# Norm factors inside the matmul operands, 512-column gate and up products and token-major z and down in the second block of a two-block transformer

## Chip, cores and metric

The kernel runs on one NeuronCore of one Trainium2 chip. The time is device microseconds of one execution. The engines are TensorE (PE, its weight loads shown apart as PEld), VectorE (DVE), ScalarE (ACT), GpSimd (POOL) and SyncE (SP), which only issues transfers here.

## The reference, cut to what matters

x has 256 tokens of 1024 channels. A first block (convolution, sparse attention, pooling, a mixture of 32 experts) makes the x that enters the second block. The change touches the second block alone:

```python
def second_block(x, c, ...):
    mod = (silu(c) @ w_ada + b_ada)
    shift1, scale1, gate1, shift2, scale2, gate2 = split(mod, 6)
    h = rms_norm(x, norm1_w) * (1.0 + scale1) + shift1
    x = x + gate1 * hybrid_mixer(h, ...)
    h = rms_norm(x, norm2_w) * (1.0 + scale2) + shift2
    x = x + gate2 * ((silu(h @ w_gate) * (h @ w_up)) @ w_down)     # D_FF = 2816
    return rms_norm(x, norm_f_w)

def hybrid_mixer(h, w_in, ...):
    p = h @ w_in
    q, k, v = split(silu(causal_depthwise_conv(p[qkv], conv_qkv_w)))  # 4 taps, 3 x 512 channels
    o = gated_delta_rule_chunked(l2_normalize(q), l2_normalize(k), v, g, beta)  # 4 heads of 128
    y_gdn = rms_norm(o, gdn_norm_w) * silu(z)                         # 512 channels
    y_sc = sc_b * causal_depthwise_conv(sc_c * sc_h, conv_short_w)    # 3 taps, 512 channels
    return concatenate([y_gdn, y_sc]) @ w_out
```

## The kernel before, in words

The whole program is one straight list of instructions. It is written in program order with tiles from pools; a scheduler orders each engine's instructions at build time by their place in the program and by its own estimate of when operands and buffers are ready, and sets all semaphores. So an engine may work on a later part of the program (a z product) while an earlier part (the delta rule) waits, but on the chip each engine keeps the order that was fixed.

Weights come through a ring of SBUF tiles of 2 MB, four of them in the second block, issued in a fixed list by SP (`pump`, L144). Six tables of modulation weights of the second block come apart from this: `ada_cols` (L1474) loads eight pieces of 512 KB into two buffers and multiplies each with the condition vector in 8 small matmuls (L1481).

Activations lie with channels on the partitions and the 256 tokens along the free dimension. Products are made in a split precision: a weight w is written as wH + wL, an activation h as hH + hL, each rounded to the fp32r type that TensorE passes once, and a product is wH hH + wL hH + wH hL. `split` (L325) makes wH by a ScalarE copy (L331) and wL by a VectorE subtraction (L332) for 128 x 512 weights at a time, with three buffers each. `prodT` (L335) makes 128 output channels for 256 tokens out of 8 slices of 128 input channels: 24 matmuls (L342, L343, L345).

The norm is a factor per token and is kept out of the operand. `scaled` (L1235) writes hH and hL of x times the channel's gain G alone; two more columns (256 and 257) hold the shift, so one product gives both the unscaled result and the shift's contribution as a column of its own. The rows of the norm factor (`rrow`, `r4row`) are multiplied onto the results on VectorE, and the shift's column is added as a bias. This is why the matmuls have 258 columns.

The mixer: `conv_silu` (L1319) makes a chunk of 128 channels of q, k or v, twelve in all. Its product lies in one of three PSUM banks `zb`; VectorE multiplies it with `rrow` into the SBUF tile `pad` (L1327), which frees the bank, and the four taps work on `pad` (L1329 ScalarE, L1331 three times VectorE); L1333 is the SiLU. The second half of each chunk's wL goes to GpSimd (`low`, L1317), as do the squares of q and k (L1355), the masked copies of the triangular inverse (L1421), one tap of the short convolution (L1598) and the low halves of the mixed operand (L1552). `rowed` (L1336) does the same for z, c, h and b, four chunks each; z is transposed to tokens afterwards (L1540). The output projection runs in two halves (`fours`, L1607) with `down` (L347), 8 blocks of 24 matmuls of 256 columns, whose moving operand is the activation.

The feed-forward part: 22 blocks of 128 hidden channels. Each makes gate and up by `prodT` (L1644, L1645) into a PSUM bank `gb` each (four of them), the hidden tile by L1658 to L1663, its split by L1666 (ScalarE) and L1667 (GpSimd), and the `down` of the block before (L1670) into four PSUM banks that hold the output with channels on the partitions. The norm factor of the second norm is worked out beside the first gate and up products (L1646 to L1655). The table for gate2 is loaded and multiplied when f is 1024 (L1640). At the end the output is added to the residual, squared, transposed back to tokens (L1689), scaled by the last norm factor (L1710, L1712) and sent out (L1713). `rsqrt` (L254) is a VectorE operation and a power on GpSimd (L257).

## Time and profile before

| what | value |
|---|---|
| median of 3 runs | 1054.34 us (1054.06 to 1055.30) |
| the profiled execution, own time | 1055.91 us |
| its span in the profile | 1053.5 us |
| TensorE busy | 871.7 us, 83% of the span |
| VectorE, ScalarE, GpSimd busy | 435.0, 328.7, 84.5 us |
| mean granted TensorE clock | 0.904 of 2.4 GHz |

The span is the time from the first to the last instruction in the profile. Busy time is the time in which an engine has at least one instruction under way. Matmuls are pipelined: a matmul of 281 ns can start 118 ns after the one before it, so the distance of starts, not the duration, tells what a matmul costs in a row of them. Columns called "idle before" name what ended the idle time.

### The profile page before, as it was taken

What the parts mean: (1) busy time and instruction counts of PE and PEld (TensorE: products, weight loads), DVE (VectorE), ACT (ScalarE), POOL (GpSimd) and SP (SyncE); (2) the same over time, 40 slices, a digit from 0 to 9 for tenths busy, and PEclk for the clock granted to TensorE, in tenths of its full rate; (3) what the DMA queues carried; (4) which work ended last, traced back from release to release, by engine and by line L of the source; (5) the groups of instructions that cost most, each with busy time, mean ns of one, the idle gap of its engine ahead of it and who ended that gap; (6) DMA issues with size and microseconds to landing.
All of it is one profiled execution on the core that took longest, in us unless ns stands there. A gap on an engine that the chain in (4) does not pass through costs nothing. (4 is left out here: it accounts for less than half of the span.)

```text
span 1053.5 us, 20710 instructions
## 1 busy us (share of the span) xinstructions
PE 871.7 (83%) x8762; PEld 635.0 (60%) x8763; DVE 435.0 (41%) x1068; ACT 328.7 (31%) x722; POOL 84.5 (8%) x109
## 2 busy tenths in 40 slices
PE   4999986986677676666665768979999999999998
PEld 3776675653333342333332326768868989989997
DVE  2599846210110010000000106585557666656665
ACT  4442744210100010000000004643425555445554
POOL 0000002000000000000000002351013010000001
PEclk9899998998888787787786888989999999999998
DMA  9999935799999999999999999422535716545521
GB/s 352 427 426 418 413 135 240 304 421 423 419 421 423 424 419 421 423 422 423 420 422 422 418 421 406 157 95 96 194 128 219 299 44 240 208 175 218 200 81 40
DMA packets 38145, 322.82 MB, mean 306 GB/s; under 512 B 4256, under 2 KB 4640, under 8 KB 9760
## 3 DMA queue, kind: packets, MB, share of 16 engines
q1 hardware_dynamic: 37584, 320.64, 74.9%
q8 instruction: 70, 1.15, 0.4%
q0 software_dynamic: 176, 0.53, 0.1%
q10 hardware_dynamic: 288, 0.29, 0.1%
q14 instruction: 27, 0.22, 0.1%
HBM read 320.38 MB, written 1.05 MB: 305 GB/s over the span
## 5 line engine op out<-in xcount | busy, mean ns | idle before, releaser
L332 DVE TENSOR_TENSOR wL<-ring,wH 128x512 fp32r<-128x512 f32 (+1 forms) x212 | 146.7, 695 | 98.6 <-ACT wH L331 98.3
L331 ACT ACTIVATE wH<-ring 128x512 fp32r<-128x512 f32 (+1 forms) x224 | 137.1, 615 | 156.4 <-PE gb L345 67.1
L1066 PE MATMUL yy<-ring,aT 128*32 128x256 f32 x992 | 95.2, 544 | 38.5 <-DMA ring<-w 38.5
L1054 DVE TENSOR_TENSOR at<-sl,hh 128x128 f32<-128x128 f32 x32 | 9.1, 285 | 243.7 <-ACT sl L1052 243.7
L1035 PE MATMUL hh<-ring,px 128*32 128x256 f32 x1024 | 75.8, 423 | 31.2 <-DMA ring<-w 30.6
L1035 PE MATMUL hh<-ring,XT 128*32 128x256 f32 x1024 | 73.6, 411 | 26.1 <-DMA ring<-w 26.0
L1066 PEld LDWEIGHTS yy<-ring,aT 128*32 128x32 f32 x992 | 43.1, 149 | 77.6 <-issue 66.0
L343 PE MATMUL gb<-mixH,wL 128*128 128x258 f32 x352 | 89.4, 285 | 0.0
L342 PE MATMUL gb<-mixH,wH 128*128 128x258 f32 x352 | 89.3, 285 | 0.0
L1035 PEld LDWEIGHTS hh<-ring,px 128*32 128x32 f32 x1024 | 31.4, 119 | 67.9 <-DMA ring<-w 43.4
L1052 ACT ACTIVATE sl<-hh 128x128 f32<-128x128 f32 x32 | 8.9, 278 | 196.7 <-PE hh L1035 196.7
L1035 PEld LDWEIGHTS hh<-ring,XT 128*32 128x32 f32 x1024 | 32.6, 116 | 59.0 <-DMA ring<-w 33.0
L343 PEld LDWEIGHTS gb<-mixH,wL 128*128 128x128 f32 x352 | 66.6, 189 | 2.5 <-issue 2.1
L342 PEld LDWEIGHTS gb<-mixH,wH 128*128 128x128 f32 x352 | 66.8, 190 | 0.8 <-ACT mixH L1236 0.8
L1072 ACT ACTIVATE px<-yy 128x256 f32<-128x256 f32 x32 | 12.3, 385 | 162.3 <-PE yy L1066 162.3
L342 PE MATMUL zb<-mixH,wH 128*128 128x258 f32 x224 | 61.1, 301 | 1.2 <-DVE pad L1327 0.6
L343 PE MATMUL zb<-mixH,wL 128*128 128x258 f32 x224 | 59.6, 293 | 0.0
L345 PE MATMUL gb<-mixL,wH 128*128 128x258 f32 x352 | 56.7, 283 | 0.0
L1048 DVE COPY MT<-tm 128x256 f32<-128x256 f32 x32 | 13.6, 424 | 98.7 <-PE tm L1046 98.7
L345 PEld LDWEIGHTS gb<-mixL,wH 128*128 128x128 f32 x352 | 48.3, 189 | 0.0
L354 PE MATMUL zb<-dd,wH 128*128 128x256 f32 x264 | 47.8, 281 | 0.0
L342 PEld LDWEIGHTS zb<-mixH,wH 128*128 128x128 f32 x224 | 44.2, 198 | 5.6 <-issue 2.1
(532 smaller groups left out, 1623.6 us busy)
## 6 DMA issues: line engine op xcount, KB each, us to landing
ring<-w SPq DMA_DIRECT2D x132, 1024.0 KB, 22.4
ring<-wall SPq DMA_DIRECT2D x35, 2048.0 KB, 10.1
ring<-w SPq DMA_DIRECT2D x29, 2048.0 KB, 24.7
ring<-wall SPq DMA_DIRECT2D x21, 1024.0 KB, 15.4
aw<-w_ada SPq DMA_DIRECT2D x32, 512.0 KB, 4.2
px<-w SPq DMA_DIRECT2D x1, 2048.0 KB, 8.2
ring<-wall SPq DMA_DIRECT2D x1, 1600.0 KB, 25.7
ring<-wall SPq DMA_DIRECT2D x1, 1536.0 KB, 25.2
```

Of the source, the lines that this page charges most:

```text
L331: nc.scalar.activation(d[0], src, AF.Copy)
L332: eng.tensor_sub(d[1], src, d[0])
L342: nc.tensor.matmul(ps, wH[:, k], h[0][:, q + k], start=(q + k == 0), stop=False)
L343: nc.tensor.matmul(ps, wL[:, k], h[0][:, q + k], start=False, stop=False)
L345: nc.tensor.matmul(ps, wH[:, k], h[1][:, q + k], start=False, stop=(q + k == 7))
L354: nc.tensor.matmul(pss[k // 2][:, 256 * (k % 2):256 * (k % 2) + 256], lw[:, c], rh, start=first and i == 0 and k % 2 == 0, stop=last and i ...
L1035: nc.tensor.matmul(ps[32 * j:32 * j + 32], XT[e // 8][:, k, e % 8, :], w[:, k % 4, :, 128 * j:128 * j + 128], start=(k == 0), stop=(k == 7))
L1048: nc.vector.tensor_copy(MT[e], ps)
L1052: nc.scalar.activation(sl, ps[:, 0], AF.Silu)
L1054: nc.vector.tensor_mul(at, sl, ps[:, 1])
L1066: nc.tensor.matmul(ps[32 * j:32 * j + 32], aT[:, 32 * c:32 * c + 32], w[:, c, 256 * j:256 * j + 256], start=(c == 0), stop=(c == 3))
L1072: nc.scalar.activation(YS[e], ps, AF.Copy)
```

## The change

- The norm factor goes into the operands: `normed` forms t = x G r (r a row per token out of PSUM) on VectorE, hH = t + S on ScalarE and hL on VectorE. Operands have 256 columns, hH and hL lie side by side, and `rrow`, `r4row`, the shift's column and all that repaired the results are gone. The two norm factors must be known before the first product of q, k and v, and of gate and up.
- `prod` (mixer) keeps 24 matmuls of 256 columns; for the first two chunks of k both products run side by side. `prod_wide` (gate and up) multiplies wH with hH and hL in one matmul of 512 columns (8), and wL with hH in one of 256 (8); the two halves of the bank are added afterwards (a ScalarE copy, a VectorE sum).
- z and the feed-forward output are made with tokens on the partitions: the activation is the weight side and 512 channels of wH or wL move. The residual is transposed to tokens inside the loop (f = 512), the gate2 row and the final norm's row are spread over the partitions ahead of the loop, and the table for gate2 is multiplied there too.
- The taps of q, k and v read the product's PSUM bank directly. The work of GpSimd named above goes to VectorE or ScalarE. `split` has six buffers in the second block instead of three, the hidden tile three instead of two. The memory of the operand tiles is freed with the first block.

```diff
-    split, prodT, down = tools(t2)
+    split, down = tools(t2, 6)
...
+    def prod_wide(pss, ws, y):
+        for q in range(2):
+            v = [split(w[:, 4 * q:4 * q + 4], 4, 128) for w in ws]
+            for k in range(4):
+                for ps, (wH, wL) in zip(pss, v):
+                    nc.tensor.matmul(ps.rearrange("p (x t) -> p x t", x=2), wH[:, k], y[q][:, :, k],
+                                     start=(q + k == 0), stop=(4 * q + k == 7), skip_group_check=True)
+            for k in range(4):
+                for ps, (wH, wL) in zip(pss, v):
+                    nc.tensor.matmul(ps[:, 0:256], wL[:, k], y[q][:, 0, k], start=False, stop=(4 * q + k == 7),
+                                     skip_group_check=True)
+
+    def normed(y, xT, G, S, rows):
+        for k in range(8):
+            t = q1("nt")
+            nc.vector.scalar_tensor_tensor(t, xT[:, k], G[:, k:k + 1], rows, op0=OP.mult, op1=OP.mult)
+            h, l = (y[k // 4][:, n, k % 4] for n in range(2))
+            nc.scalar.activation(h, t, AF.Identity, bias=S[:, k:k + 1])
+            nc.vector.scalar_tensor_tensor(l, t, S[:, k:k + 1], h, op0=OP.add, op1=OP.subtract)
...
+    def conv_silu(dst, ps, chunk):
         cv = q1("cv")
-        nc.scalar.activation(cv, pad[:, 3:], AF.Copy, scale=P("cqkv", 4 * chunk + 3))
-        for t in range(3):
-            nc.vector.scalar_tensor_tensor(cv, pad[:, t:t + 256], P("cqkv", 4 * chunk + t), cv,
+        nc.scalar.activation(cv, ps, AF.Copy, scale=P("cqkv", 4 * chunk + 3))
+        for t in (2, 1, 0):
+            nc.vector.scalar_tensor_tensor(cv[:, 3 - t:], ps[:, 0:253 + t], P("cqkv", 4 * chunk + t), cv[:, 3 - t:],
...
-            nc.gpsimd.tensor_mul(sqh.rearrange("p (a t) -> p a t", a=2), raw[n][:, :, h], raw[n][:, :, h])
+            nc.scalar.activation(sqh.rearrange("p (a t) -> p a t", a=2), raw[n][:, :, h], AF.Square)
...
-        nc.gpsimd.tensor_mul(Ls, LT, GK("mT")[:, None, 64 * lev:64 * lev + 64].to_broadcast([128, 8, 64]))
+        nc.vector.tensor_mul(Ls, LT, GK("mT")[:, None, 64 * lev:64 * lev + 64].to_broadcast([128, 8, 64]))
...
+    pss = [zb(), zb()]
+    for k in range(8):
+        wH, wL = split(wz[:, k], 1, 512)
+        for a in range(2):
+                r = slice(128 * a, 128 * a + 128)
+                h, l = (y3[k // 4][:, n, k % 4, r] for n in range(2))
+                nc.tensor.matmul(pss[a], h, wH, start=(k == 0), stop=False)
+                nc.tensor.matmul(pss[a], l, wH, start=False, stop=False)
+                nc.tensor.matmul(pss[a], h, wL, start=False, stop=(k == 7))
...
-        nc.gpsimd.tensor_sub(mview(mL, k), src, mview(mH, k))
+        nc.vector.tensor_sub(mview(mL, k), src, mview(mH, k))
...
+    r4 = t2.tile([128, 2], F32, name="r4")
+    rsqrt(r4, pst[:, 0:2], 1.0 / D)
+    tok_row(pst[:, 256:512], r4)
+    y4 = ytiles()
+    normed(y4, x3T, G4, S4, pst[:, 256:512])
...
+    R = ada_sums(5120, ps)
...
     for f in range(0, 2816, 512):
-        if f == 1024:
-            ada_cols(5120, gt2, P("ab2", 8, 8), gb)
...
-            prodT(pg[:, 0:258], wg, 128 * j, y4)
-            prodT(pu[:, 0:258], wu, 128 * j, y4)
...
+                prod_wide([pg], [wg[:, :, c]], y4)
+                prod_wide([pu], [wu[:, :, c]], y4)
...
+            nc.scalar.activation(low[:, 0:256], pg[:, 256:512], AF.Copy)
+            nc.vector.tensor_add(tg, pg[:, 0:256], low[:, 0:256])
+            nc.scalar.activation(tg, tg, AF.Silu)
+            nc.scalar.activation(low[:, 256:512], pu[:, 256:512], AF.Copy)
+            nc.vector.tensor_add(tu, pu[:, 0:256], low[:, 256:512])
+            nc.vector.tensor_mul(hd, tu, tg)
...
-            nc.gpsimd.tensor_sub(dL, hd, dH)
...
+            nc.vector.tensor_sub(dd[:, 256:512], hd, dd[:, 0:256])
...
+    for a in range(2):
+        for c in range(2):
+            for n, (_, d) in enumerate(pend):
+                down2(halves_[n], d, a, c, False, n == 1)
+            r = slice(512 * c, 512 * c + 512)
...
+            nc.vector.tensor_mul(t, acc[a][c], gtr[:, r])
+            nc.vector.tensor_add(x4[a][:, r], x4[a][:, r], t)
...
+            nc.scalar.activation(t, x4[a][:, r], AF.Square, accum_out=ss5[:, a, c:c + 1])
+        nc.vector.tensor_add(r5[:, a:a + 1], ss5[:, a, 0:1], ss5[:, a, 1:2])
+        rsqrt(r5[:, a:a + 1], r5[:, a:a + 1], 1.0 / D)
...
+            nc.vector.scalar_tensor_tensor(x4[a][:, r], x4[a][:, r], r5[:, a:a + 1], nfr[:, r],
+                                           op0=OP.mult, op1=OP.mult)
+            nc.sync.dma_start(outv[:, a, r], x4[a][:, r])
```

## Rows read from the trace of the kernel before

**Rows 1.** The page, busy time of an engine (share of the span) and instructions.
```profile
PE 871.7 (83%) x8762; PEld 635.0 (60%) x8763; DVE 435.0 (41%) x1068; ACT 328.7 (31%) x722; POOL 84.5 (8%) x109
```
**Rows 2.** Busy time of each engine in stretches of the second block.
```profile
core 0: us, PE busy (x) PEld busy (x) DVE busy (x) ACT busy (x) POOL busy (x), PEclk, DMA share, GB/s
640.00:658.00 18.00, 16.10 (x128) 13.24 (x121) 13.86 (x49) 9.58 (x23) 6.32 (x5) 0.81 0.95 398
658.00:724.00 66.00, 56.07 (x676) 47.88 (x678) 45.45 (x96) 36.31 (x85) 28.08 (x24) 0.95 0.29 108
724.00:840.50 116.50, 116.50 (x1090) 96.77 (x1080) 69.58 (x160) 49.33 (x105) 13.96 (x18) 1.00 0.56 202
840.50:854.50 14.00, 12.31 (x97) 10.24 (x96) 9.39 (x24) 7.60 (x17) 1.54 (x2) 1.00 0.34 130
906.00:945.00 39.00, 39.00 (x333) 33.90 (x332) 21.54 (x44) 17.38 (x31) 2.94 (x4) 1.00 0.60 234
945.00:1039.50 94.50, 94.50 (x789) 94.50 (x789) 62.02 (x121) 50.25 (x88) 7.76 (x11) 1.00 0.39 145
```
**Rows 3.** TensorE: timeline, one line's matmuls, and the chain (start us, us, what).
```profile
110.62 1.03 PE L690 MATMUL bank<-kvT,qaT 128*128 128x256 f32 x4
...
L1149 PE MATMUL pb<-par,S x16: 256/256/276, 644.5 to 646.2; 128*128 128x8 f32 x16
...
644.50 1.95 PE L1149 MATMUL pb<-par,S 128*128 128x8 f32 x16
...
L633 PE MATMUL bank<-cqT,ring x16: 379/379/483, 102.3 to 106.4; 128*128 128x256 f32 x16
...
L354 PE MATMUL zb<-dd,wH 128*128 128x256 f32 x264 | 47.8, 281 | 0.0
...
857.33 1.66 PE zb L354 x14
```
**Rows 4.** Groups of VectorE and ScalarE in 945 to 1039.5 us.
```profile
L332 DVE TENSOR_TENSOR wL<-ring,wH 128x512 fp32r<-128x512 f32 x66 | 47.5, 719 | 30.0 <-ACT wH L331 30.0
L1663 DVE SCALAR_TENSOR_TENSOR hd<-tu,bgu,sl 128x256 f32<-128x256 f32 x11 | 5.3, 484 | 1.1
...
L331 ACT ACTIVATE wH<-ring 128x512 fp32r<-128x512 f32 x66 | 41.6, 630 | 40.3 <-PE gb L345 32.1 <-PE ax L354 7.5 <-ACT wH L331 0.7
```
**Rows 5.** Timeline from the output projection to the second gate; the page's modulation loads.
```profile
841.31 0.87 DVE L1613 SCALAR_TENSOR_TENSOR x1T<-ax,gt,x1T 128x256 f32<-128x256 f32 x2
...
849.91 1.15 POOL L257 TENSOR_TENSOR r<-r,mhalf 128x2 f32<-128x2 f32 x1 [30.16 <-DVE r L256]
851.12 0.43 PE L320 MATMUL gb<-kon,r 128*128 128x128 f32 x2 [1.69 <-DVE wL L332]
851.59 0.39 ACT L1655 ACTIVATE r4row<-gb 128x256 f32<-128x256 f32 x1 [1.31 <-PE gb L320]
...
854.49 0.16 DVE L1658 COPY bgu<-gb 128x1 f32<-128x1 f32 x1
...
aw<-w_ada SPq DMA_DIRECT2D x32, 512.0 KB, 4.2
```
**Rows 6.** 658 to 724 us: TensorE's longest wait, GpSimd and VectorE ahead of it.
```profile
PE gb L1407 <- DVE TT L1415: 4.2, 1, 4.2
...
688.38 3.19 POOL L1421 TENSOR_TENSOR Ls<-LT,hk 128x512 f32<-128x512 f32 x2 [0.26 <-DVE LT L1399]
...
691.77 1.75 DVE L1415 SCALAR_TENSOR_TENSOR TT<-TT,par 128x512 f32<-128x512 f32 x1
...
L332 POOL TENSOR_TENSOR wL<-ring,wH 128x512 fp32r<-128x512 f32 x12 | 15.5, 1296 | 27.1 <-ACT wH L331 23.6 <-DVE pv L1277 3.3 <-ACT pad L1326 0.2
```
**Rows 7.** Timeline of the end: the last down matmul and the last scaling.
```profile
1042.82 0.28 PE L354 MATMUL ax<-dd,wL 128*128 128x256 f32 x1
...
1048.27 1.41 DVE L1710 TENSOR_SCALAR xf<-gb,r 128x512 f32<-128x512 f32 x2 [1.98 <-PE gb L1689]
```
**Rows 8.** Timeline of the first k chunk: its last matmuls and last tap.
```profile
653.35 0.95 PE L345 MATMUL zb<-mixL,wH 128*128 128x258 f32 x4
...
659.82 0.47 DVE L1331 SCALAR_TENSOR_TENSOR cv<-pad,par,cv 128x256 f32<-128x256 f32 x1
```

More of the change, by code (lines that the diff above doesn't have):

```diff
@@ L356, in down @@
                                      skip_group_check=True)
-        return split, prodT, down
+        return split, down
     ss1 = fr.tile([128, 2], F32, name="ss1")
@@ L793, in build @@
     nc.gpsimd.memset(oneb, 1.0)
-    split, prodT, down = tools(fr)
+    split, down = tools(fr, 3)
     rwG = fr.tile([128, 8, 36], F32, name="rwG")
@@ new lines, in normed, with ytiles @@
+    def normed(y, xT, G, S, rows):
[5 more added lines that the diff above has]
+            nc.vector.scalar_tensor_tensor(l, t, S[:, k:k + 1], h, op0=OP.add, op1=OP.subtract)
+    def ytiles():
+        return [t2.tile([128, 2, 4, 256], F32R, name=f"y{i}") for i in range(2)]
@@ L1246, in build @@
+    y3 = ytiles()
     rows = gb()
     tok_row(rows[:, 0:256], rr[:, :, 1])
-    rrow = t2.tile([128, 256], F32, name="rrow")
-    nc.scalar.activation(rrow, rows[:, 0:256], AF.Copy)
+    normed(y3, x2T, G3f, S3, rows[:, 0:256])
     x3T = x2T
@@ L1643, in build @@
             pg, pu = gb(), gb()
[L1644 to L1645 removed]
+            c = slice(128 * j, 128 * j + 128)
             if f + j == 0:
[L1647 to L1655 removed]
@@ L1691, in build @@
-    for half in range(2):
-        for n, b in enumerate(pend):
-            down(pss, *b, False, n == 1, range(4 * half, 4 * half + 4))
-    pst = None
-    for half in range(2):
-        last(half)
-        if pst is None:
-            pst = zb()
-        for n in range(4 * half, 4 * half + 4):
-            for a in range(2):
-                for j in range(2):
-                    nc.tensor.matmul(pst[64 * j:64 * j + 64, a:a + 1], sq[n][:, 128 * a + 64 * j:128 * a + 64 * j + 64],
-                                     ones[:, 0:1], start=(n == 0 and a == 0), stop=(n == 7), skip_group_check=True)
+                prod_wide([pg, pu], [wg[:, :, c], wu[:, :, c]], y4)
+            else:
+                prod_wide([pg], [wg[:, :, c]], y4)
+                prod_wide([pu], [wu[:, :, c]], y4)
@@ new lines, in build @@
+            if f == 512 and j < 2:
+                for b in range(2):
+                    ps = gb()
+                    for i in range(4):
+                        nc.tensor.transpose(ps[:, 128 * i:128 * i + 128], x3T[:, 4 * b + i, 128 * j:128 * j + 128],
+                                            ident)
+                    nc.scalar.activation(x4[j][:, 512 * b:512 * b + 512], ps, AF.Copy)
+    outv = A["out"].rearrange("(a p) d -> p a d", p=128)
+    ss5 = t2.tile([128, 2, 2], F32, name="ss5")
```

239 lines of the change are left out of this document (99 added, 140 removed).

## The prediction

> **What bounds the kernel now.** I read the page first: TensorE is busy 83% of the span, GpSimd 8% [rows 1]. A busy share says little of a pipelined engine, so the table by stretch is next [rows 2]. The second block is everything after about 640 us. From 724 to 840.5 us and from 906 to 1039.5 us TensorE has no idle time at the full granted clock. In the last stretch it starts 789 matmuls in 94.5 us, one every 0.120 us. One block of 128 feed-forward columns has 24 gate, 24 up and 24 down matmuls, so a block costs 72 x 0.120 = 8.64 us; there are 22. VectorE is at 66% there and ScalarE at 53%: they wait for TensorE. Between 658 and 724 us it is different: TensorE idles 9.9 of 66 us, VectorE works 45.5 us and GpSimd 28.1 us. Around 840.5 to 854.5 us and after 1043 us there are two short serial stretches. After 658 us the weight transfers take 0.29 to 0.60 of the DMA engines, so they are not the bound. The change touches only the second block; the 640 us before it stay.
>
> **The feed-forward loop.** The change turns 32 of the 48 gate and up matmuls into 16 with 512 columns and leaves 16 with 256; the 24 down matmuls become 12 with 512. That is 28 wide and 16 narrow starts instead of 72, with the same columns. No row shows an fp32r matmul with 512 columns. Nearest is an fp32 one with 256 columns: it takes 379 ns where the fp32r one with 256 takes 281, about one more pass over its columns [rows 3]. Four in a row start (1.03 - 0.379)/3 = 0.217 us apart, so one pass of 512 columns should start every 0.217 us. A matmul with 8 columns but a full 128-column weight load starts every (1.95 - 0.276)/15 = 0.112 us: a weight load can stand beside a pass of 0.217 us, while at 256 columns (0.120) the two are nearly equal and neither hides the other quite. A narrow one costs what it does now in a run of 14, 1.66/14 = 0.118 us. I take 0.220 for a wide one, nearer the fp32 row, since it streams as long; the other bound is that columns alone cost, 2 x 0.118 = 0.236 us. A block is then 28 x 0.220 + 16 x 0.118 = 8.05 us, and the loop wins 22 x 0.59 = **13 us**. The bounds are 15.5 us (0.217, 7.96 us less rounding) and 3 us (0.236, 8.50 us).
>
> The Trainium skill's page TensorE: Matmul & The Clock Gate, section Back-to-back issue gap, puts a warm gap at N/2.4 + 2.5 ns, which is 109 ns for 256 and 216 ns for 512 columns. By it merging two matmuls gives back 2.5 ns and the loop would win about 2 us; the trace's 0.120 us at 256 columns does not agree with 109, so I keep the row and hold the reading that columns alone count as a rival.
>
> Can the other engines follow at 8.05 us? Per block VectorE now works 62.0/94.5 x 8.64 = 5.7 us. It loses two copies of 0.16 and keeps three operations of 0.4 to 0.5, and takes the low half of the hidden tile from GpSimd (about 0.4): 5.8 us [rows 4]. ScalarE has 4.6 us and gains two copies out of PSUM (about 0.39 each): 5.4 us. Both stay under 75%, and the split tiles go from three to six buffers. So this costs nothing as long as TensorE stays the slowest; if a split were late, it would cost its own 0.6 to 0.7 us.
>
> **The start of the feed-forward part.** Before, the first product starts as soon as single residual columns are there, and the norm factor is multiplied in afterwards. After, the factor stands ahead of the operands. From the last output-projection matmul (840.5): the four residuals 1.8, square and token sums 0.7, rsqrt 0.17 + 1.15 on GpSimd, the row transposes 0.43, first product and copy 1.0: the first gate matmul starts at +5.3 us [rows 5]. Then VectorE sets the pace, with two operations of 0.48 per k (as L1663 in [rows 4]): 8 x 0.96 = 7.7 us, and the first gate and up end at +13.7, the second gate at +16.4. Now the second gate's result is first read at 854.49, +13.9. In terms of lost TensorE time that is 8.3 us (16.4 less 8.1 of products) against 5.3 (13.9 less 8.64). The last modulation product (64 small matmuls over eight loads) moves from the loop to just before it. In 906 to 945 us it costs 39 - 267 x 0.120 = 7.0 us [rows 2], and the change adds the broadcast of its result (8 x 0.217 = 1.7) and takes 16 transposes from the end into the loop (16 x 0.11 = 1.8). So 8.3 + 8.7 + 1.8 stands against 5.3 + 7.0, +6.5 us less what falls into the 8.3 us hole. The weights come in pieces with two buffers and 4.2 us to land, so about four turns of that; I take half of the hole filled, 4.5 us. Net **+2 us**, between -2 (all filled) and +6.5 (none). On SP these eight loads now stand ahead of the ring loads that wait for the first gate block's buffers; at a DMA share of 0.34 that is free, as are two row loads on ScalarE's queue that are read only at the end, and scratch tiles that move into one pool of six.
>
> **The mixer.** The products lose two columns of 258: 576 x 2 ns = 1.2 us (0.118 for 0.120). z becomes 48 x 0.220 = 10.6 us for 96 x 0.120 plus eight transposes = 12.4: together -3 us, from -1 to -4. GpSimd's part goes to VectorE and ScalarE: twelve weight lows (1.30 us each on GpSimd, 0.69 on VectorE) and five masked copies (1.5, then about 0.69) early on, eight lows of the mixed operand (about 0.4 each) after 724 us, where VectorE has 47 us to spare; the squares of q and k go to ScalarE. VectorE loses per chunk a tiny product and a scaling (0.57), and it stops being stretched: beside two GpSimd operations of 3.19 us together, and the next, L1415 took 1.75 us and stands before TensorE's longest wait, 4.2 us [rows 6]. Sum for VectorE between 648 and 724 us: +8.3 + 3.4 + 7.7 (the normed operands) - 6.8 - about 10 of stretch, so nearly zero. Nothing excludes a loss; the waits of 9.9 us can shrink by at most themselves. I take -3 us for them, between -7 and +6. The mixer's own start is paced by the same 7.7 us; now its first two chunks run there at a granted clock that averages 0.81 [rows 2], and at half clock 48 matmuls of 256 columns take 10 us anyway. So zero, from -2 to +3. Mixer **-6 us**. GpSimd keeps the powers of the rsqrts and the clearing of one tile, so "without GpSimd" is not meant of those.
>
> **The end.** The output now falls out by token. After the last matmul: product 0.68, sum 0.69, square 0.8, rsqrt 1.1 with GpSimd, two scalings of 0.7 and waits: about 5.2 us. Before, the last scaling ends at 1049.7, 6.6 us after the last down matmul; the 3.8 us of output transfer behind it stay [rows 7]. **-1.3 us**, from 0 to -2.
>
> Sum: -13 + 2 - 6 - 1.3 = -18.3 us. The profiled execution takes 1055.9 us, its span 1053.5 and 2.4 around it, and lies 1.6 us over the median of the runs. So 1054.3 - 18.3 = **1036 us**.
>
> **Rivals.**
> - Columns alone count (0.236 us a wide matmul). For it: 0.120 us at 256 columns is more than the weight load's 0.112, so something besides the load costs. Against it: the fp32 row at 0.217. Then -3 instead of -13: 1046 us.
> - VectorE becomes the bound of the mixer: what GpSimd did stands in its queue behind the normed operands, and the waits between 658 and 724 us grow by 6 instead of shrinking by 3, and no hole is filled at the feed-forward start (+4.5). For it: 45.5 of 66 us are busy there. Against it: the stretching ends. 18.3 - 13.5 = 5 us are left: 1049 us.
> - Slower: the chunk's PSUM bank. Now a q, k or v chunk frees its bank after one scaling; then it holds it until the last of four tap operations. Three banks and 2.83 us a product allow 2 x 2.83 = 5.7 us after a chunk's last matmul. In the trace the first chunk's matmuls end at about 654.3 and its last tap at 660.3, 6.0 us later [rows 8], and z holds two of the three banks. Twelve chunks that each stall TensorE by more than 1.5 us over the limit (a hold above 7.2 us) eat all that is won; at 2 us it is 12 x 2 = 24 us and 1060 us. Against it: without interleaved GpSimd stretches the taps take 1.4 + 0.5 us, and one late chunk is not twelve.
> - Everything falls well: 0.217 us, the hole filled, the waits gone: -28 us, 1026 us.
>
> **Numbers.** Forecast 0.60, columns alone 0.12, VectorE bound 0.12, banks 0.08, all well 0.08. The forecast's own range is 1029 to 1044 us. With the two middling rivals and the lower end the range is 1026 to 1050. Three runs spread by 0.12%, so 0.2% (2.1 us) is about what can be told from no change. Faster 0.87, same 0.04, slower 0.09.
>
> **What would show it.** In the after profile: wide matmuls 0.215 to 0.222 us apart and a block of about 8.0 us; TensorE without idle time in the loop; a first gate product about 5 us after the last output projection, with the last modulation's matmuls in that hole; no wait of 4 us behind L1415's operation; about 9 us from the last matmul to the end. Wide matmuls at 0.236, tap operations as the releaser of the products, or gate and up matmuls that wait for a split or a load would prove it wrong.

## The result, and the profile after

The changed kernel takes **1065.56 us** (median of 4 runs, 1061.26 to 1068.95); the kernel before, run beside it, 1054.20 us (1052.80 to 1055.30). The ratio is 1.0100, 95% interval 1.0079 to 1.0121: slower by about 11 us, where the prediction said 1036 us and held 1026 to 1050 us for its range. The profiled execution took 1063.87 us, its span 1062.2 us, 8.7 us more than the span before. The account by stages below explains these 8.7 us; what the medians have beyond them (11.4 us) is spread between executions of one kernel.

The page's line on the engines, to set beside [rows 1]:

```profile
PE 866.8 (82%) x8078; PEld 600.5 (57%) x8079; DVE 431.3 (41%) x1025; ACT 342.1 (32%) x760; POOL 23.9 (2%) x44
```

GpSimd fell from 84.5 to 23.9 us, and the number of matmuls by 684. TensorE's busy time fell by only 5 us. The change did what it says; the time is in the stretches. The windows view of the changed kernel has the columns of [rows 2]; from the third row on the borders are put where the same work begins and ends:

```profile
640.00:658.00 18.00, 11.13 (x87) 9.34 (x77) 14.03 (x45) 9.42 (x19) 1.96 (x2) 0.72 0.95 400
658.00:724.00 66.00, 60.09 (x645) 49.81 (x643) 45.54 (x98) 41.63 (x90) 3.28 (x2) 1.00 0.34 126
724.00:842.30 118.30, 112.10 (x1120) 92.79 (x1119) 61.46 (x128) 47.80 (x98) 2.01 (x2) 0.97 0.59 212
842.30:862.80 20.50, 12.87 (x110) 5.83 (x108) 9.64 (x24) 5.87 (x14) 0.70 (x1) 0.58 0.47 154
945.00:1043.70 98.70, 98.70 (x521) 84.42 (x520) 64.91 (x117) 57.96 (x117) 0.00 (x0) 1.00 0.36 139
1043.70:1062.20 18.50, 5.84 (x27) 4.41 (x25) 9.93 (x19) 3.69 (x10) 1.10 (x2) 0.77 0.15 57
```

Three things stand out against [rows 2]. From 724 us to the last output projection TensorE had no idle time; now it idles 6.2 us there. Between 842.3 and 862.8 us lies a stretch that the kernel before hasn't got: 20.5 us in which TensorE has 110 matmuls, at a granted clock of 0.58. And the loop, 945 to 1043.7 us, is as full as before.

Where the second block's time went, by the start times of four matmuls in the timeline (the same table is used for the experiments below; each row is one profiled execution):

| kernel | first mixer product at | to last output projection | to first gate | to last down | to the end |
|---|---|---|---|---|---|
| before | 648.7 | 191.8 | 0.1 | 202.2 | 10.7 |
| after | 648.2 | 194.1 | 20.4 | 186.4 | 13.1 |

So -0.5 + 2.3 + 20.3 - 15.8 + 2.4 = +8.7 us. Of the 15.8 us that the feed-forward part won, 7 are the last modulation product, which went to its start.

**The loop.** The chain of waits, through one block (start us, us, what):

```profile
987.99 0.92 PE gb L1222 x4
988.91 0.48 PE gb L1226 x4
...
993.59 0.23 PE zb L1662
993.82 0.23 PE zb L1663
...
996.38 0.92 PE gb L1222 x4
```

Four 512-column gate matmuls take 0.92 us, a down matmul of 512 columns 0.23, four of 256 columns 0.48. From one block's first matmul to the next one's are 8.39 us (987.99 to 996.38), where it was 8.64.

**The start of the feed-forward part.** TensorE's timeline from the last output projection (L341) to the first gate product (L1222); in brackets the idle time ahead and what ended it:

```profile
842.31 0.28 PE L341 MATMUL ax<-mH,wL 128*128 128x256 f32 x1
842.51 1.07 PE L1464 MATMUL gb<-aw,cs 128*32 128x256 f32 x16
843.51 1.41 PE L1616 MATMUL gb<-ones,sqx 128*64 128x1 f32 x32
846.80 1.08 PE L1464 MATMUL gb<-aw,cs 128*32 128x256 f32 x8 [1.88 <-DMA aw<-w_ada]
847.81 0.69 PE L320 MATMUL gb<-kon,r 128*128 128x128 f32 x2
...
851.33 1.08 PE L1464 MATMUL gb<-aw,cs 128*32 128x256 f32 x8 [1.81 <-DMA aw<-w_ada]
853.62 1.08 PE L1464 MATMUL gb<-aw,cs 128*32 128x256 f32 x8 [1.22 <-DMA aw<-w_ada]
855.78 1.08 PE L1464 MATMUL gb<-aw,cs 128*32 128x256 f32 x8 [1.07 <-DMA aw<-w_ada]
858.02 1.08 PE L1464 MATMUL gb<-aw,cs 128*32 128x256 f32 x8 [1.16 <-DMA aw<-w_ada]
859.60 3.50 PE L1646 MATMUL gb<-aR,kon 128*128 128x256 f32 x8 [0.50 <-ACT aR L1467]
862.75 2.21 PE L1222 MATMUL gb<-y,wH 128*128 128x512 f32 x8
```

The row of the norm factor (L320) is out at 848.5 us, 6.2 us after the last output projection; its operand was ready at 845.9 us, and a piece that waited for its load stood ahead of it. The order fixed at build time puts all eight pieces of the modulation product (L1464) and the spreading of its result (L1646) ahead of the first gate. Two pieces are there when it comes to them; of the other six, five wait for a transfer that could start only when a buffer came free (the one left out, at 848.43 us, doesn't). TensorE waits, its clock falls to half (0.50 granted from 847.8 to 859.6 us), and even the spreading takes 3.50 us.

**The waits** of TensorE between 640 and 860 us (us in total, times, longest):

```profile
PE gb L1464 <- DMA aw<-w_ada: 7.1, 5, 1.9
PE ax L1464 <- DMA aw<-w_ada: 5.3, 3, 2.7
PE zb L1210 <- DVE cv L1316: 3.9, 4, 1.4
PE zb L1211 <- DVE y L1236: 3.4, 1, 3.4
PE zb L1210 <- ACT y L1235: 2.2, 1, 2.2
```

The 4.2 us wait of [rows 6] is gone. In its place stand modulation loads in the mixer too (`ax`), four waits for the taps that read a product's PSUM bank (L1316), and the normed operand. The mixer as a whole, from its first product to the last output projection, in the windows view of the kernel before (first row) and of the changed kernel (second row, and its beginning):

```profile
648.70:840.48 191.78, 181.85 (x1813) 153.93 (x1814) 122.50 (x281) 89.85 (x198) 45.08 (x45) 0.97 0.49 178
648.20:842.31 194.11, 178.62 (x1790) 148.74 (x1790) 116.37 (x256) 94.69 (x198) 5.29 (x4) 0.96 0.52 191
648.20:658.00 9.80, 6.43 (x29) 6.13 (x30) 9.35 (x31) 5.26 (x11) 0.00 (x0) 0.51 0.91 379
```

TensorE is busy 3.2 us less and idle 5.6 us more (15.5 instead of 9.9). With the rows above the idle time has three places: 3.4 us more up to 658 us, 4.0 us less from there to 724 us (5.9 instead of 9.9), 6.2 us more behind it.

**The end.** VectorE's timeline after the last down matmul, which starts at 1049.14 us:

```profile
1048.18 0.69 DVE L1715 TENSOR_TENSOR low<-zb,gtr 128x512 f32<-128x512 f32 x1 [1.98 <-PE zb L1664]
1048.90 0.69 DVE L1716 TENSOR_TENSOR x<-x,low 128x512 f32<-128x512 f32 x1
...
1052.83 0.69 DVE L1715 TENSOR_TENSOR low<-ax,gtr 128x512 f32<-128x512 f32 x1
1053.45 1.41 DVE L1723 SCALAR_TENSOR_TENSOR x<-x,r,nfr 128x512 f32<-128x512 f32 x2
1054.79 0.69 DVE L1716 TENSOR_TENSOR x<-x,low 128x512 f32<-128x512 f32 x1
...
1057.33 1.41 DVE L1723 SCALAR_TENSOR_TENSOR x<-x,r,nfr 128x512 f32<-128x512 f32 x2 [0.67 <-POOL r L257]
```

Twelve operations of 128x512 stand in one queue. The last sum (1054.79) waits behind two scalings of the other 128 tokens.

### The profile page after: what moved, and what is told of

The parts are those of the page before. It is cut to its first block, busy times and chain, and to the rows that moved or that the text cites. A ratio compares the mean times of both kernels' runs of the same rounds, so it can differ in the third digit from the quotient of the medians.

```text
span 1062.2 us, 19258 instructions
## 1 busy us (share of the span) xinstructions
PE 866.8 (82%) x8078; PEld 600.5 (57%) x8079; DVE 431.3 (41%) x1025; ACT 342.1 (32%) x760; POOL 23.9 (2%) x44
## 4 chain that ended last, share of the span: by engine, by line
PE 47%; DMA 45%; DVE 4%; ACT 2%; issue 1%; POOL 0%; DVEq 0%; POOLq 0%; SPq 0%; ACTq 0%
DMA ring<-w 38%; PE gb L1222 8%; PE gb L1226 4%; DMA ring<-wall 3%; DMA aw<-w_ada 3%; PE zb L1210 2%; PE zb L1211 2%; PE zb L1214 2%; PE zb L341 2%; PE hh L1022 1%; PE zb L1662 1%; PE zb L1664 1%; PE zb L1663 1%; PE gb L1389 1%; PE mod L223 1%
## 5 line engine op out<-in xcount | busy, mean ns | idle before, releaser
L331 DVE TENSOR_TENSOR wL<-ring,wH 128x512 fp32r<-128x512 f32 (+1 forms) x224 | 149.7, 672 | 107.0 <-ACT wH L330 96.1
L1222 PE MATMUL gb<-y,wH 128*128 128x512 f32 x352 | 95.7, 393 | 0.0
L1222 PEld LDWEIGHTS gb<-y,wH 128*128 128x128 f32 x352 | 61.5, 188 | 9.5
L1226 PEld LDWEIGHTS gb<-y,wL 128*128 128x128 f32 x352 | 53.9, 188 | 7.4
L1210 PE MATMUL zb<-y,wH 128*128 128x256 f32 x192 | 50.6, 298 | 6.8 <-DVE cv L1316 3.9
L1226 PE MATMUL gb<-y,wL 128*128 128x256 f32 x352 | 56.0, 282 | 0.0
L1035 DVE COPY MT<-tm 128x256 f32<-128x256 f32 x32 | 13.6, 424 | 96.6 <-PE tm L1033 96.6
L1211 PE MATMUL zb<-y,wH 128*128 128x256 f32 x192 | 49.5, 292 | 3.4 <-DVE y L1236 3.4
L1065 PE MATMUL acc<-MT,px 32*128 32x256 f32 x512 | 42.6, 440 | 7.2 <-PEq L1089 4.7
L1210 PEld LDWEIGHTS zb<-y,wH 128*128 128x128 f32 x192 | 37.5, 198 | 10.8 <-issue 3.5
L1065 PEld LDWEIGHTS acc<-MT,px 32*128 32x128 f32 x512 | 26.3, 208 | 24.9 <-issue 13.8
L1211 PEld LDWEIGHTS zb<-y,wH 128*128 128x128 f32 x192 | 37.5, 198 | 4.1 <-DVE y L1236 3.7
```

The costliest lines, as they stand in the source:

```text
L331: nc.vector.tensor_sub(v[1], src, v[0])
L1035: nc.vector.tensor_copy(MT[e], ps)
L1065: nc.tensor.matmul(acc[j][:, i], YS[e][r, 128 * i:128 * i + 128], MT[e][r], start=(e == 0 and i == 0), stop=(e == 31), skip_group_check=True)
L1210: nc.tensor.matmul(ps, wH[:, k], y[q][:, 0, k], start=(q + k == 0), stop=False)
L1211: nc.tensor.matmul(ps, wH[:, k], y[q][:, 1, k], start=False, stop=False)
L1222: nc.tensor.matmul(ps.rearrange("p (x t) -> p x t", x=2), wH[:, k], y[q][:, :, k], start=(q + k == 0), stop=(4 * q + k == 7), skip_group_c ...
```

## The experiments

Theory: the change lost its gain to four separate things: a 512-column matmul costs nearly two of 256; the modulation product now waits for its loads on the path to the first gate; VectorE has too much in the mixer; the end is a queue on VectorE. The rivals differ from run to run. The kernels were timed in several groups, each on one chip beside runs of the kernel before; across groups the ratios to the kernel before are the safer comparison.

### Gate2 back in the loop

```diff
-    ps = gb()
-    R = ada_sums(5120, ps)
...
     for f in range(0, 2816, 512):
+        if f == 1024:
+            ps = gb()
+            R = ada_sums(5120, ps)
...
```

> The changed kernel, with the last modulation product and its broadcast put back into the loop at f = 1024. Theory A (its eight loads, two at a time, stand in TensorE's fixed order ahead of the first gate matmul): the first gate starts about 7 us after the last output-projection matmul instead of 20.4, the loop grows by 8 to 9 us, and the time falls by 4 to 6 us against the changed kernel, to about 1060. Theory B (the operands that wait for the norm factor hold the start by themselves): the first gate still starts 13 us or more after it, and the time rises by 1 to 4 us, to about 1068.

Measured: 1075.12 us (4 runs), ratio 1.0195 (1.0177 to 1.0214) to the kernel before. The gap ahead of the first gate fell from 20.4 to 7.1 us, as theory A had it, but the stretch behind it grew by 23 us and not by 8 to 9: neither theory had the time. TensorE's timeline of this kernel, in the loop:

```profile
932.00 2.31 PE L1464 MATMUL gb<-aw,cs 128*32 128x256 f32 x16 [5.52 <-DMA aw<-w_ada]
936.74 1.08 PE L1464 MATMUL gb<-aw,cs 128*32 128x256 f32 x8 [2.44 <-DMA aw<-w_ada]
```

So 13 us of the gap are the modulation product, and 7 are the norm chain. The move back doesn't give the old loop back, though: in the kernel before the same eight pieces were spread over 906 to 940 us and waited for no load; here they stand within 920 to 939 us and wait 10.2 us. So two buffers alone don't make the stall, nor does the place alone; with two buffers it comes where the pieces stand close together. Why the scheduler packs them tighter here was not tried.

### Five modulation buffers

```diff
-    split, down = tools(t2, 6)
+    split, down = tools(t2, 3)
...
-            w = t2.tile([128, 1024], F32, name="aw", bufs=2)
+            w = t2.tile([128, 1024], F32, name="aw", bufs=5)
```

> The changed kernel with five buffers for the pieces of the modulation weights instead of two, paid with three split buffers instead of six. Theory A: TensorE's waits for these pieces (7.1 us at the feed-forward start, 5.3 us in the mixer) fall under 3 us together, the two stretches at half clock get shorter, and the time falls by 9 to 14 us, to about 1054. Theory B: the waits fall but the first gate stays near 13 us behind the output projection, since the operands are not ready: the time falls by 3 to 6 us. If three split buffers are too few, gate and up wait for their splits and the loop's block grows above 8.5 us.

Measured: 1055.73 us (10 runs), ratio 1.0016 (1.0005 to 1.0027): by the ratios some 9 us of the 11 are back. (Its profiled execution, 1052.86 us, is the fastest of the ten.) The time is near theory A's, the gap is theory B's: 13.6 us, and the waits on loads there are down from 7.1 to 1.7 us. In the mixer these waits are gone (5.3 us before), but it is only 1.6 us shorter, since TensorE then waits 4.3 us for the delta rule's normed output (0.5 us in the changed kernel). From the timeline of the gap:

```profile
844.56 0.98 PE L1464 MATMUL gb<-aw,cs 128*32 128x256 f32 x8 [1.34 <-DMA aw<-w_ada]
845.90 2.31 PE L1464 MATMUL gb<-aw,cs 128*32 128x256 f32 x16 [0.36 <-DMA aw<-w_ada]
848.72 3.38 PE L1646 MATMUL gb<-aR,kon 128*128 128x256 f32 x8 [0.50 <-ACT aR L1467]
```

The split buffers could be halved at no visible cost: the block stays at 8.39 us.

### Gate and up with 256 columns

```diff
-                prod_wide([pg], [wg[:, :, c]], y4)
+                prod([pg[:, 0:256]], [wg[:, :, c]], y4)
...
-            nc.scalar.activation(low[:, 0:256], pg[:, 256:512], AF.Copy)
-            nc.vector.tensor_add(tg, pg[:, 0:256], low[:, 0:256])
-            nc.scalar.activation(tg, tg, AF.Silu)
+            nc.scalar.activation(tg, pg[:, 0:256], AF.Silu)
```

> The changed kernel with gate and up as 24 matmuls of 256 columns each, so that the copies and sums of the two bank halves go away. Columns alone count (a wide matmul starts every 0.232 us in the trace): a block costs 16 x (2 x 0.119 - 0.232) = 0.1 us more, the loop 2 us, the time about 1067. A wide matmul at 0.220 as forecast: 22 x 0.29 = 6 us more, 1071. If the added copies and sums were what limits the loop: less than the changed kernel, 1060 to 1064.

Measured: 1068.82 us, ratio 1.0137 (1.0118 to 1.0157), 3.3 us over the changed kernel's median. The chain of this kernel has gate matmuls of 0.12 us, four in 0.48, beside down matmuls of 512 columns:

```profile
991.91 0.23 PE ax L1664
992.14 0.12 PE gb L1210
...
993.09 0.48 PE gb L1214 x4
...
997.84 0.23 PE zb L1662
```

A block takes 8.49 us instead of 8.39 (the distance of the blocks' first gate matmuls). Merging 32 matmuls into 16 is thus worth 0.10 us a block, 2.2 us over 22 blocks. That columns cost, and the number of matmuls hardly, is shown.

### GpSimd's part of q, k and v given back

```diff
-            v = [split(w[:, 4 * q:4 * q + 4], 4, 128) for w in ws]
+            v = [split(w[:, 4 * q:4 * q + 4], 4, 128, eng[q]) for w in ws]
...
-            nc.scalar.activation(sqh.rearrange("p (a t) -> p a t", a=2), raw[n][:, :, h], AF.Square)
+            nc.gpsimd.tensor_mul(sqh.rearrange("p (a t) -> p a t", a=2), raw[n][:, :, h], raw[n][:, :, h])
...
-        nc.vector.tensor_mul(Ls, LT, GK("mT")[:, None, 64 * lev:64 * lev + 64].to_broadcast([128, 8, 64]))
+        nc.gpsimd.tensor_mul(Ls, LT, GK("mT")[:, None, 64 * lev:64 * lev + 64].to_broadcast([128, 8, 64]))
```

> The changed kernel with GpSimd's part of the q, k and v stage given back: the second half of the weight lows, the masked copies and the squares. If GpSimd held the mixer up (long operations and the stretching of VectorE's): the stretch from the first product to the first output-projection matmul grows by 3 to 6 us, the time to about 1070. If VectorE's larger load is what kept the mixer from shrinking: it falls by 2 to 5 us, to about 1062.

Measured: 1065.05 us, ratio 1.0109 (1.0090 to 1.0127), as the changed kernel. But the mixer is 4.5 us shorter (189.6 us), and the gap behind it 2.3 us longer (22.7): TensorE reached the modulation loads earlier and waited for them longer (9.3 instead of 7.1 us). So half of the gain was lost in a wait on transfers; in this execution the first mixer product also came 1.1 us later, and the stretch behind the first gate took 1.0 us more.

### Gate2 with the other modulation tables, five buffers

```diff
     nc.vector.scalar_tensor_tensor(G4, G4, 1.0, P("n2w2"), op0=OP.add, op1=OP.mult)
+    R = ada_sums(5120, ax())
...
     for f in range(0, 2816, 512):
+        if f == 1024:
+            for b in range(2):
+                pr = gb()
...
```

> Kernel after with five modulation buffers (three split buffers), and the eight pieces of the gate2 product multiplied right behind the other three modulation tables of the mixer; only the spreading of the result over the partitions stays in the loop (f = 1024). Theory (the start of the feed-forward part is long because the modulation product stands between output projection and first gate, on top of the norm chain): the gap between the last output-projection matmul and the first gate matmul falls from 13.5 us (same buffers, product at the start) to 7 us, as it was with the product in the loop; the mixer takes the 64 small matmuls, free if they fall into its waits, up to 5 us if not. Time 1049 to 1054 us. Rival (the gap is the norm chain alone, the product hides in it): the gap stays at 12 to 14 us, and the time rises by what the mixer takes, 1056 to 1061 us.

Measured: 1051.71 us (12 runs), ratio 0.9971 (0.9960 to 0.9983), 4.0 us below the run with five buffers alone. The gap is 7.3 us, and the mixer takes 193.7 us with the extra 64 matmuls in it, no more than the 194.1 of the changed kernel. TensorE's timeline shows what is left of the gap:

```profile
843.66 1.44 PE L1617 MATMUL gb<-ones,sqx 128*64 128x1 f32 x32 [0.91 <-ACT sqx L1609]
846.14 0.69 PE L320 MATMUL gb<-kon,r 128*128 128x128 f32 x2 [1.04 <-POOL r L257]
849.76 3.78 PE L1222 MATMUL gb<-y,wH 128*128 128x512 f32 x8 [2.93 <-DVE y L1236]
```

The squares, the rsqrt and the first normed operand, 0.91 + 1.04 + 2.93 us of waits. Then the first eight gate matmuls start 0.45 us apart (849.76 to 853.34), nearly twice 0.23, at half clock (0.50 granted).

### The same with the two buffers of the change

The edit is that of the run before, with `aw` at 2 and `tools(t2, 6)`.

> Kernel after with its two modulation buffers and six split buffers, and the gate2 product moved behind the other three tables of the mixer. Tells place from buffers. Theory (each pair of pieces costs a turn of the transfers wherever it stands, because TensorE's order is fixed): gap at the start of the feed-forward part 7 us instead of 20.4, but 5 to 10 us more in the mixer; 1058 to 1064 us. Rival (only the place counts, the mixer has time for the turns): gap 7 us, mixer unchanged, 1052 us.

Measured: 1062.82 us, ratio 1.0102 (1.0070 to 1.0135), no other than the changed kernel's 1.0100. The gap is 7.3 us, but the mixer takes 201.2 us, 7 us more than in the changed kernel. Its waits for modulation loads there:

```profile
PE ax L1464 <- DMA aw<-w_ada: 5.7, 5, 2.4
```

The time is the theory's, its reason only in part: the four tables wait 5.7 us here, the three of the changed kernel 5.3, and the pieces of gate2 wait 1.4 us. About 3.6 us of the 7 are the 64 matmuls themselves (64 x 0.057 us, their distance in a row at full clock), and the rest is not told apart. Against the run before, with the same place and five buffers, the mixer is 7.5 us longer and the time 11 us. So with two buffers the new place gives nothing that can be told from the old one, and with five it is worth 4 us.

### GpSimd's part given back, with the gate2 product out of the way

The edits of the last two kinds together (five buffers).

> As the run before, and GpSimd's part of the q, k and v stage is given back (half the weight lows, squares, masked copies). Theory (VectorE, with GpSimd's work on top, stretches the mixer by 3 to 4 us, and in the earlier run this was given back only because the modulation loads set the start of the feed-forward part): first mixer product to last output projection 3 us or more shorter than in the run before, and this time the run is 3 us shorter too. Rival (GpSimd's slow operations on the same SBUF stretch VectorE's own, so nothing is won): within 1 us of the run before.

Measured: 1048.49 us (6 runs), ratio 0.9945 (0.9925 to 0.9965), 3.2 us below the run without it, as the theory had it. What was hidden in the earlier run now shows. TensorE's waits for the taps fall from 5.3 us in three to 0.5 us in one. That the taps were late because VectorE also made the weights' low halves is not shown: in the earlier run with the same work given back they were still 5.1 us in three, and the edit moves lows, masked copies and squares (from ScalarE) together. VectorE's own operation got slower (the mean of its weight lows between 658 and 724 us rises from 685 to 822 ns beside GpSimd's of 1325), and the stage is faster all the same. The largest wait left in this kernel's mixer, and its place in the timeline:

```profile
PE gb L1570 <- DVE yg L1564: 4.1, 1, 4.1
PE zb L1210 <- DVE cv L1316: 0.5, 1, 0.5
...
783.37 1.54 PE L1570 MATMUL gb<-kon,yg 128*128 128x128 f32 x6 [4.08 <-DVE yg L1564]
```

### Short convolution ahead of the transposes

TensorE waits there for the normed output of the delta rule, with the c, h and b products queued behind the transposes. The program order of the two is exchanged (on top of the run before):

```diff
-    for h in range(0, 4, 2):
-        ps = gb()
...
     x3_out()
     wc_, wh_, wb_ = get("w2i_c"), get("w2i_h"), get("w2i_b")
...
+    for h in range(0, 4, 2):
+        ps = gb()
...
```

> As e6_early_pool, and in the program the short convolution (its c, h and b products) stands ahead of the transposes of the normed delta-rule output, so that TensorE's fixed order has products to work on while VectorE makes that output. Theory (z by token and the c products were pulled ahead of the delta rule, nothing is left to cover its end: TensorE waits 4.1 us for VectorE's yg and then runs about 10 us at the lower of its two clocks): the wait goes and the clock stays up, the mixer is 4 to 8 us shorter, the time 1041 to 1045 us. Rival (the work only changes places, and the mixed operands are then late for the output projection): within 1.5 us of 1048.5.

Measured: 1045.46 us (4 runs), ratio 0.9911 (0.9896 to 0.9926), 3.0 us lower. The mixer falls from 190.4 to 185.3 us. The wait for yg is gone; a smaller one took its place:

```profile
783.06 0.39 PE L1210 MATMUL zb<-y,wH 128*128 128x256 f32 x1 [2.08 <-ACT u L1576]
```

The granted clock of 776 to 792 us rises from 0.68 to 0.89. It doesn't stay at full speed, which the theory expected: the time is 0.5 us above its range, and far from the rival's.

### Two tries at the end

The first gives two of four additions to GpSimd (on top of the gate2 run):

```diff
-            nc.vector.tensor_add(x4[a][:, r], x4[a][:, r], t)
+            (nc.vector, nc.gpsimd)[c].tensor_add(x4[a][:, r], x4[a][:, r], t)
```

> As e5_early, and two of the four residual additions behind the last down matmul go from VectorE to GpSimd. Theory (the end is a serial chain on VectorE, 4 products, 4 additions and 4 scalings of 0.7 us after the last matmuls): VectorE loses 2 x 0.69 = 1.4 us, but GpSimd takes longer for each than VectorE, so the stretch from the last down matmul to the end falls by 0.5 to 1.4 us, from 13.1. Rival (the end is set by the output transfer or the norm factor): no change within 0.3 us.

Measured: 1052.62 us (12 runs), ratio 0.9982 (0.9971 to 0.9993), 0.9 us above the run without it; the end is 13.5 instead of 13.1 us. The two intervals overlap. GpSimd takes 1.26 and 1.67 us for what takes 0.69 on VectorE, and VectorE waits for it. (The Trainium skill's GPSIMD Engine Reference, section Engine selection, calls GpSimd about two times slower for such operations; the trace agrees, with 1.8 and 2.4 times.) Timelines of GpSimd and VectorE in this kernel:

```profile
1039.26 1.26 POOL L1716 TENSOR_TENSOR x<-x,low 128x512 f32<-128x512 f32 x1 [194.50 <-ACT low L1718]
...
1040.55 0.69 DVE L1715 TENSOR_TENSOR low<-zb,gtr 128x512 f32<-128x512 f32 x1 [1.44 <-POOL x L1716]
```

The second, on top of the short-convolution run, takes two scalings out of VectorE's way:

```diff
+            if a == 0:
+                nc.scalar.activation(x4[a][:, r], x4[a][:, r], AF.Copy, scale=r5[:, a:a + 1])
+                (nc.gpsimd, nc.vector)[c].tensor_mul(x4[a][:, r], x4[a][:, r], nfr[:, r])
+            else:
```

> As e9_conv_first, and the final scaling of the first 128 tokens is split into a ScalarE scaling by the norm factor and a product with the norm's gain, half of it on GpSimd, half on VectorE, so that VectorE's last addition no longer waits behind two scalings of 0.7 us. Theory (VectorE's order sets the end): the stretch from the last down matmul to the end falls from 13.1 by 0.7 to 1.4 us. Rival (the output transfers or the squares on ScalarE set it): within 0.3 us, or worse by up to 1 us as GpSimd holds the second norm factor back.

Measured: 1044.44 us (5 runs), ratio 0.9905 (0.9888 to 0.9922). The end takes 12.7 instead of 13.1 us. VectorE's last addition does come 1.2 us earlier, counted from the last down matmul, but the product behind it, beside GpSimd's, takes 1.26 us and holds the second norm factor back:

```profile
1034.46 0.69 DVE L1716 TENSOR_TENSOR x<-x,low 128x512 f32<-128x512 f32 x1
1035.72 1.26 DVE L1725 TENSOR_TENSOR x<-x,nfr 128x512 f32<-128x512 f32 x1 [0.57 <-ACT x L1724]
```

Neither try found what the theory promised. That VectorE's queue sets the end is read from the timeline, and not shown by a shorter one.

### Work for the gap

```diff
-            if f == 512 and j < 2:
...
+    x4 = [m4("x4", "T5"), m4("x4", "T6")]
+    for b in range(2):
+        pr = gb()
...
+    for j in range(2):
+        for b in range(2):
+            ps = gb()
...
     acc = [[zb(), zb()], [zb(), ax()]]
```

> As e10_tail_pool, and two pieces of work that stand in the loop and wait for no load (the spreading of gate2 over the partitions, and the 16 transposes of the residual) are put between the output projection and the first gate product, where TensorE waits 7 us for the norm factor and the normed operand. Theory (the hole left there is the norm chain, and work that needs no transfer falls into it free): the gap stays at 7 to 8.5 us, the loop is 3 to 3.5 us shorter, the time 2 to 3.5 us lower. Rival (ScalarE's four copies of the transposes and the extra work stand ahead of the normed operand, and the gap grows by what the loop loses): within 1 us of e10_tail_pool.

Measured: 1044.16 us (4 runs), ratio 0.9892 (0.9875 to 0.9908), the best kernel of the study, though not told apart from the run before it. The loop is 3.3 us shorter, as the theory had it; the gap is 8.7 instead of 7.0 us, the output projection 1.0 us longer, since half of the spreading fell into it, and in its execution the first mixer product was 2.9 us later, a place that the edit doesn't touch. By the time alone the rival holds, by the stages the theory does; what separates the two is smaller than the spread of the runs.

### The kernel before with gate2 early

```diff
-            w = t2.tile([128, 1024], F32, name="aw", bufs=2)
+            w = t2.tile([128, 1024], F32, name="aw", bufs=3)
...
+    ada_cols(5120, gt2, P("ab2", 8, 8), ax)
...
-        if f == 1024:
-            ada_cols(5120, gt2, P("ab2", 8, 8), gb)
```

> The kernel before with the one thing that helped the changed kernel most: the gate2 table multiplied with the other three tables in the mixer, here with three modulation buffers (there is no room for five). Theory (the kernel before has no wait on these loads, so it has little to win): its loop loses 7 us and the mixer takes 4 to 8 us, so 1051 to 1056 us, no change within 3 us. Rival (the place of this product was as costly before): 1046 to 1049 us, and then the changed kernel with the same care is no faster than this one.

Measured: 1050.57 us (8 runs), ratio 0.9961 (0.9948 to 0.9974). The loop loses 7.3 us, the mixer takes 4.4. It lies 0.4 us under the theory's range and 1.6 us above the rival's: the move helps the kernel before by 4.5 us (1055.11 to 1050.57). So the mended change is to be set against 1050.6 us rather than 1055: it is 6 us faster, not 11. Of the other repairs, a different order around the delta rule's end was not tried on the kernel before, so it isn't shown that all of these 6 us belong to the change.

The stages of all runs, as in the table above:

| kernel | median us | mixer | to first gate | to last down | to the end |
|---|---|---|---|---|---|
| gate2 in the loop | 1075.12 | 196.4 | 7.1 | 209.5 | 13.1 |
| five buffers | 1055.73 | 192.5 | 13.6 | 186.4 | 13.1 |
| 256 columns | 1068.82 | 195.4 | 21.9 | 189.6 | 13.1 |
| GpSimd back | 1065.05 | 189.6 | 22.7 | 187.4 | 13.1 |
| gate2 early, two buffers | 1062.82 | 201.2 | 7.3 | 190.7 | 13.1 |
| gate2 early, five buffers | 1051.71 | 193.7 | 7.3 | 190.9 | 13.1 |
| that, two additions on GpSimd | 1052.62 | 193.9 | 7.3 | 189.4 | 13.5 |
| that, GpSimd back | 1048.49 | 190.4 | 7.1 | 190.1 | 13.1 |
| that, short convolution first | 1045.46 | 185.3 | 7.1 | 189.7 | 13.1 |
| that, end split | 1044.44 | 186.8 | 7.0 | 190.0 | 12.7 |
| that, gap filled | 1044.16 | 186.8 | 8.7 | 186.7 | 12.7 |
| before, gate2 early | 1050.57 | 196.2 | 0.1 | 194.9 | 10.2 |

Where gate2 is spread in the loop, one block takes 10.12 us instead of 8.39, and behind the gap of 7 us the first gate products run at half clock: this is why "to last down" is 190 there and 186.4 where the spreading stands ahead of the loop. Most executions of a kernel lie within 4 us of their median (one of gate2 early with two buffers 9 us above), so small differences in one cell are not read.

## Why the prediction was wrong

The prediction's sum was -13 + 2 - 6 - 1.3. By the two traces the terms came out as -5.5 + 10 + 2.3 + 2.4, and the mixer began 0.5 us earlier: +8.7 us.

- **The loop, predicted -13, measured -5.5** (22 blocks by 8.64 - 8.39). The failing step: "I take 0.220 for a wide one, nearer the fp32 row, since it streams as long". A wide matmul starts every 0.231 us, a narrow one every 0.119 to 0.120: merging two gives back 2 x 0.119 - 0.231 = 7 ns (9 with 0.120), not 20. With these, 28 x 0.231 + 16 x 0.120 = 8.39 us, the block as it was measured. (The best case of the loop, 15.5 us, was also wrongly summed: 22 x 0.676 is 14.9.) The fp32 row of [rows 3] was one row of four matmuls, too little to lean on against the bound of 0.236. The rival "columns alone count" had the mechanism and a block of 8.50. Beside it the formula N/2.4 + 2.5 ns of the Trainium skill's page TensorE: Matmul & The Clock Gate, section Back-to-back issue gap, was the better guide in kind (little comes back from merging), though not in figure: its 216 ns is not met by 231. The page gives it for an isolated matmul and about 131 ns for 512 columns in a real kernel, which the prediction left out; the measured 231 ns is further from that. That TensorE has no idle time in the loop, and that VectorE and ScalarE follow, held.
- **The start of the feed-forward part, predicted +2 (bounds -2 to +6.5), measured +10.** From the last output projection to the last down matmul the time went from 202.3 to 206.8 us, +4.5, though the loop's blocks won 5.5. The failing step: "about four turns of that; I take half of the hole filled". Four turns of 4.2 us are 17 us, and I counted them as matmul time of a hole 8.3 us long instead of as time in which TensorE, in a fixed order, can do nothing else. In the trace 16.6 us pass from the first piece (842.51) to the end of the last (859.1), and then 3.5 us of spreading at half clock. (Three turns were waited for, since the first two pieces had landed; they took 4.5 to 5.5 us each.) The norm chain itself was nearly right: 7.1 us to the first gate where 5.3 was said, once nothing else stands there. With five buffers the same stretch takes 200.0 us: -2.3 = -5.5 + 3.2, near the predicted +2. The bound "none filled" was thus no bound, since work that waits for loads can make the hole longer. The prediction weighed the loads' place in SP's queue and the DMA share, and missed that each turn needs a buffer that TensorE has to free first.
- **The mixer, predicted -6, measured +2.3.** Its terms were -3 for the products, -3 for the waits between 658 and 724 us (-7 to +6) and nothing for its start (-2 to +3). The first two held: TensorE was busy 3.2 us less, and its waits between 658 and 724 us fell by 4.0. VectorE's sum, "so nearly zero", held too (59.3 us busy between 640 and 724 us before, 59.6 after), and the rival of VectorE as the bound didn't come as it was stated, with waits that grow by 6. The failing step is the two stretches that it put at nothing. The start came out at its upper bound: TensorE is idle 3.4 us more up to 658 us, in a wait for the normed operand (L1236). And the stretch behind 724 us had no term at all, because TensorE had no wait there and VectorE "47 us to spare": it now has 6.2 us of waits, 5.3 of them on modulation loads, which the kernel before, with its other order, didn't wait for. So -3.2 + 3.4 - 4.0 + 6.2 makes the +2.3, but for rounding. Taking away one of these waits didn't give back its size: with five buffers the 5.3 us on modulation loads were gone, and the mixer was 1.6 us shorter. GpSimd's part given back was worth 3.2 us of the time (1051.71 to 1048.49) and the order around the delta rule's end 3.0 us; nothing in the prediction looked at what else would cover that end. The slower rival, a chunk's PSUM bank held by its taps, was there at four chunks and 1 us each, not at twelve and 2 us. With all repairs the mixer takes 185.3 us (186.8 in two later kernels with the same mixer), 5 to 6.5 less than before and with 64 matmuls more in it: the predicted size could be had, but not by the change alone. The wait of [rows 6] did go, but it didn't come back either when GpSimd's masked copies did (0.5 us in that kernel), so the reason I gave for it is not borne out.
- **The end, predicted -1.3 (0 to -2), measured +2.4.** The failing step counted one product, one sum and one square after the last matmul. All four quarters of the output become ready within 1.4 us, so four products, four sums and four scalings queue on VectorE: from the end of the last down matmul (1049.54) to the last scaling's end (1058.74) are 9.2 us, where 5.2 were counted and the kernel before took 6.6. That this queue sets the end is read from the timeline; the two tries to shorten it didn't show it.

The chances were wrong as a whole: 0.87 for faster rested on four terms that each had its own way to fail, and only one rival, with 0.08, led to a slower kernel.

## What to carry to other kernels

Ahead of moving work into a hole, ask what it waits for: an engine with a fixed order stops at the first load that isn't there, and with two buffers pieces that stand close together cost turns of the transfer (7.1 us of waits at the start, 10.2 in the loop; none in the kernel before, where they stood 34 us apart from first to last). Where one engine's work is given to another, look at what the receiving engine's queue releases, and at what the moved work had been covering. And a gain ahead of such a wait can stay invisible until the wait is gone (GpSimd's part: 0.5 us before, 3.2 us after), so an idea that "does nothing" is worth a second run behind the next repair.

## What the runs showed of the hardware

- An fp32r matmul of 512 columns behind a 128-column weight load starts every 0.231 us at full clock, one of 256 every 0.119 us: 3% between one wide and two narrow.
- After a stretch in which TensorE waits much, its next products pay too: eight 512-column gate matmuls 0.45 us apart behind the 7 us gap (granted clock 0.50), and 0.231 in the loop (1.00).
- VectorE's operations got longer where GpSimd worked beside them (1.26 us for a product of 128x512 where others of that size took 0.69; weight lows from 685 to 822 ns), and still the mixer got 3.3 us shorter when GpSimd took nearly half of the lows between 658 and 724 us at 1.33 us each, the masked copies and the squares.
